# Stores of scan operands begun by ScalarE's queue instead of SyncE's

## The chip, the cores and the metric

The kernel runs on one core of a Trainium2 chip. The core has TensorE (PE, matrix products), VectorE (DVE), ScalarE (ACT), GpSimd (POOL) and SyncE (SP), which here only begins transfers (DMAs). Each engine works through its own list of instructions in order; an instruction waits until the semaphores that it names are high enough, and all behind it on that engine wait too. A DMA is begun by the engine in whose list it stands: `nc.sync.dma_start` is SyncE, `nc.scalar.dma_start` is ScalarE. The metric is the device time in microseconds (us).

## The reference, cut to what matters

One inference step through two layers, over 128 context tokens and 1024 latent tokens: an attention layer with an MLP, and then a bidirectional RWKV-7 layer with an MLP. The change lies in the second layer's time mixing:

```
xr, xw, xk, xv, xa, xg = (h + xx * mu[n] for n in range(6))
r = (xr @ w_rkv[0]).reshape(hs)
k = (xk @ w_rkv[1]).reshape(hs)
v = (xv @ w_rkv[2]).reshape(hs)
...
for d in range(2):
    wlog = -softplus(-(w0[d] + tanh(xw @ w1[d]) @ w2[d])) - 0.5
    decay = exp(-exp(wlog))
    a = sigmoid(a0[d] + (xa @ a1[d]) @ a2[d])
    kd = k * (1.0 + (a - 1.0) * k_a)
    y, sf = wkv_scan(r, decay, kd, v, kk, a, s0[:, d], reverse=(d == 1))
```

The scan is a recurrence over tokens: S = S * w - (S kk) (kk a)^T + v k^T, y = S r, for 16 heads of 64 in each direction.

## The kernel before, in words

All 1152 tokens are held as 9 tiles of 128 or 3 blocks of 384, and as 18 chunks of 64 for the scan. Features lie in 8 groups p8 of 128 (two heads). The RWKV layer has two stages: `rwkv_proj` makes projections and operands, `rwkv_scan` runs the recurrence.

`rwkv_proj` runs a row of dense projections (`dense`, `gemm`, line 1113, tiles rp): for r (`dense(0)`) and for v (`dense(2)`), 24 outputs of 128x384 each, every one 24 matmuls of split weights pwh and pwl. ScalarE copies each out of PSUM (L1118, ro) and begins its store (L1119); for v the block is also transposed on TensorE (L1209, vp), copied (L1211, vt) and stored (L1212). While these run, the generator `operands()` is stepped every second projection. It goes over 8 groups p8 and 3 blocks b, and in each over two directions d: 48 steps. A step is, with the names that the rows show:

- on TensorE two small projections lp (L1176), which give the decay and the rate before their nonlinearities;
- on ScalarE cum (tanh, L1262), ec (L1263) and tha (L1266);
- on VectorE the scan over the chunk (L1264);
- on ScalarE the exponentials en and ec (L1268, L1269), the chunk's decay Dc (L1270) and kd (L1276);
- on GpSimd the two halves of ar (L1272, L1273), kd times k (L1277) and half of bk (L1281); on VectorE tha times kk (L1278) and the other half of bk (L1280);
- on TensorE 48 small products ng of bk and ar (L1292): the diagonal blocks of 32 x 32; on VectorE nt (L1294), their masked copy.

At the start of a block k, kk and r are loaded (L1227, L1247), into a ring of six buffers (tag ld); VectorE scales kk (L1249). After both directions GpSimd adds the two kd (L1300), VectorE multiplies them with r (L1301), and TensorE sums over heads (hst, L1126). Once the third of the inputs of v is mixed, three of four steps keep cum, en, tha and so on in a spare large tile, and the rows then call them es. ar, bk and ld have two, two and six buffers. A step ends with its stores: ar to ard (384 KB, L1274), bk to bkd (384 KB, L1282), nt to nd (64 or 96 KB, L1298), and in the first block of a group also the first two chunks to ndp (32 KB, L1297). That is 48 + 48 + 48 + 16 = 160 stores. After a group's last block, for the first three groups, the diagonal blocks are loaded back (L1346) and inverted on VectorE (L1351, L1352).

`rwkv_scan` later loads ard and bkd (L1433 to L1439) and runs the recurrence.

What stands in which place of an engine's list is decided when the kernel is built, by a planner that plays the program through a model of the chip (`schedule_with_timeline_sim=True`). It also picks the buffers of a ring. So an edit on one engine can move instructions on all.

Of the kernel before, what the change touches and what calls it, by code (L numbers as in the profile page):

```python
# [58 lines left out]
def heads(ap):  # L59

    return ap[:, None].to_broadcast([2, 64, ap.shape[-1]])
# [28 lines left out]
class Net:  # L90
# [932 lines left out]
    def rwkv_proj(self, act, early, pool, pse, ps):  # L1023
        A, S, V, G, T, dma, dr = self.A, self.S, self.V, self.G, self.T, self.dma, self.dr
        KE = (V, G)[KDE]
        NC, NB = TOK // 64, 6
# [95 lines left out]
        def head_sums(x, out):  # L1122

            sp = ps.tile([128, 3, 2], F32, tag="st", name=self.nm("hst"), bufs=1)
            for t in range(3):
                T.matmul(sp[:, t], x[:, t * 128 : (t + 1) * 128], ones2, start=True, stop=True)  # L1126
            V.tensor_copy(out.rearrange("p e t -> p t e"), sp)
# [39 lines left out]
        def second_weights(n, p8):  # L1167

            w = pool.tile([128, 128], F32, tag="w2", name=self.nm("w2"), bufs=4)
            src = A[{1: "rwkv_w2", 4: "rwkv_a2", 5: "rwkv_g2"}[n]][0]  # L1170
            dma(w, (src if n == 5 else src.rearrange("d r n -> (d r) n"))[:, p8 * 128 : p8 * 128 + 128])
            return w

        def second(n, w, b, r):
            p = pse.tile([128, HW], F32, tag="lp", name=self.nm("lp"), bufs=3)[:, 0:TB]
            T.matmul(p, w[r], tl[n, b][r], start=True, stop=True)  # L1176
            return p
# [36 lines left out]
        def etiles():  # L1214

            nonlocal turn
            turn = (turn + 1) % 4 if len(vs) == 3 else 0
            if turn:
                t = self.act_pool.tile([128, KD * HW], F32, tag=f"acta{turn - 1}", name=self.nm("es"))
                it = iter(t[:, i * NB * 65 : (i + 1) * NB * 65] for i in range(6))  # L1220
                return lambda nme, w=TB: next(it)[:, 0:w]
            return lambda nme, w=TB: pool.tile([128, NB * 65], F32, tag="e", name=self.nm(nme), bufs=EB)[:, 0:w]

        def load(src, nme):
            t = pool.tile([128, TB], F32, tag="ld", name=self.nm(nme), bufs=LB)
            if src is not None:
                dma(t, src)  # L1227
            return t

        def operands():  # L1230


            nm = pool.tile([128, 32], F32, name="nm")
            for e in range(2):
                for i in range(2):
                    r = slice(64 * e + 32 * i, 64 * e + 32 * i + 32)
                    dma(nm[r], self.C["gmask"][r, 0, e, 32 * i : 32 * i + 32])
            self.tri = {}
            ndp = self.tri[KD] = dr.tile([KD, 2, 2, 2, 2, 32, 32], F32, name="ndp")
            for p8 in range(KD):  # L1240
                ww, wa = second_weights(1, p8), second_weights(4, p8)
                for b in range(3):
                    ts = slice(b * TB, (b + 1) * TB)
                    cs = slice(b * NB, (b + 1) * NB)
                    k = load(rkd[1][:, p8, ts], "k")
                    kk = load(None, "kk")
                    dma(kk, heads(kkd[p8, :, ts]))  # L1247
                    r = load(rkd[0][:, p8, ts], "r")
                    V.scalar_tensor_tensor(kk, k, self.CB[:, 80 + p8 : 81 + p8], kk, op0=ALU.mult, op1=ALU.mult)  # L1249
                    kds = None  # L1250
                    for d in range(2):
                        etile = etiles()
                        inc = slice(1, 65) if d == 0 else slice(0, 64)
                        exc = slice(0, 64) if d == 0 else slice(1, 65)
                        pad = slice(0, 1) if d == 0 else slice(64, 65)
                        last = slice(64, 65) if d == 0 else slice(0, 1)
                        st = 1 if d == 0 else -1
                        cw, ca = 48 + d * 8 + p8, 64 + d * 8 + p8
                        ec = etile("ec", NB * 65).rearrange("p (c t) -> p c t", t=65)
                        c_ = etile("cum", NB * 65).rearrange("p (c t) -> p c t", t=65)  # L1260
                        G.memset(ec[:, :, pad], 0.0)
                        S.activation(c64(c_[:, :, :].rearrange("p c t -> p (c t)")[:, 0:TB]), c64(second(1, ww, b, row(d))), AF.Tanh, bias=hb[:, cw : cw + 1], scale=0.5)  # L1262
                        S.activation(ec[:, :, inc], c64(flat(c_)[:, 0:TB]), AF.Copy, scale=-0.5 * KAP, bias=-0.5 * KAP)  # L1263
                        V.tensor_tensor_scan(flat(c_)[:, ::st], flat(m01), flat(ec)[:, ::st], 0.0, op0=ALU.mult, op1=ALU.add)  # L1264
                        tha = etile("tha")
                        S.activation(tha, second(4, wa, b, row(d)), AF.Tanh, bias=hb[:, ca : ca + 1], scale=0.5)  # L1266
                        en = etile("en")
                        S.activation(c64(en), c_[:, :, inc], AF.Exp, scale=-1.0)  # L1268
                        S.activation(flat(ec), flat(c_), AF.Exp)  # L1269
                        S.activation(self.Dc[:, p8, d, cs, None], c_[:, :, last], AF.Exp)  # L1270
                        ar = pool.tile([128, 2, NB, 64], F32, tag="ar", name=self.nm("ar"), bufs=2)
                        G.tensor_tensor(ar[:, 0], c64(kk), ec[:, :, exc], op=ALU.mult)  # L1272
                        G.tensor_tensor(ar[:, 1], c64(r), ec[:, :, inc], op=ALU.mult)  # L1273
                        dma(self.ard[d][p8, :, :, cs], ar)  # L1274
                        kd = etile("kd")
                        S.activation(kd, tha, AF.Identity, scale=hb[:, 88 + p8 : 89 + p8], bias=oka[:, p8 : p8 + 1])  # L1276
                        KE.tensor_tensor(kd, kd, k, op=ALU.mult)  # L1277
                        V.scalar_tensor_tensor(tha, tha, 1.0, kk, op0=ALU.add, op1=ALU.mult)  # L1278
                        bk = pool.tile([128, 2, NB, 64], F32, tag="bk", name=self.nm("bk"), bufs=2)
                        V.scalar_tensor_tensor(bk[:, 0], c64(tha), 0.5, c64(en), op0=ALU.mult, op1=ALU.mult)  # L1280
                        (V, G)[BKE].tensor_tensor(bk[:, 1], c64(kd), c64(en), op=ALU.mult)  # L1281
                        dma(self.bkd[d][p8, :, :, cs], bk)  # L1282
                        if b == 0 and d == 0:
                            nd = dr.tile([2, NC - 2, 2, 2, 32, 32], F32, name=self.nm("nd"))

                        ng = ps.tile([128, NB, 32], F32, tag="ng", name=self.nm("ng"), bufs=1)
                        for j in range(NB):
                            for e in range(2):
                                x, z = (bk, ar) if d == 0 else (ar, bk)
                                for i in range(2):  # L1290
                                    t = slice(32 * i, 32 * i + 32)
                                    T.matmul(ng[64 * e + 32 * i : 64 * e + 32 * i + 32, j], x[row(e), 0, j, t], z[row(e), 0, j, t], start=True, stop=True, tile_position=(64 * e, 64 * e + 32 * i))  # L1292
                        nt = etile("nt", TB // 2).rearrange("p (c t) -> p c t", t=32)
                        V.tensor_tensor(nt, ng, nm[:, None, :].to_broadcast([128, NB, 32]), op=ALU.mult)  # L1294
                        m = 2 if b == 0 else 0
                        if m:
                            dma(ndp[p8, d].rearrange("c e i s t -> (e i s) c t"), nt[:, 0:m])  # L1297
                        dma(nd[d, b * NB + m - 2 : b * NB + NB - 2].rearrange("c e i s t -> (e i s) c t"), nt[:, m:])  # L1298
                        kds = kd if d == 0 else (kds, kd)
                    G.tensor_tensor(kds[0], kds[0], kds[1], op=ALU.add)  # L1300
                    V.scalar_tensor_tensor(kds[0], r, self.CB[:, 96 + p8 : 97 + p8], kds[0], op0=ALU.mult, op1=ALU.mult)  # L1301
                    head_sums(kds[0], bss[:, p8, :, 3 * b : 3 * b + 3])
                    if b == 2:
                        self.tri[p8] = nd
                        if p8 < PI:
                            for _ in self.invert(pool, p8):
                                pass
                    yield
# [584 lines left out]
```

## Time and profile before

| | us |
|---|---|
| median of 3 runs (4411.51 to 4431.69) | 4413.0 |
| profiled execution, its own time | 4424.38 |
| span of its trace, first to last instruction | 4422.6 |
| busy in the span: TensorE, VectorE, ScalarE, GpSimd | 3968.7, 2764.0, 1713.0, 1231.5 |

The operands are made from about 2263 to 2755 us of the span, some 490 us. The profile has rows by stretch (how long each engine was busy), waits (which engine idled for which instruction of which other), and a timeline (start in us, duration in us, engine, line, operation, output<-input, and in brackets the idle time just before with its cause). SPq and ACTq are DMAs begun by SyncE and ScalarE; the time of such a row is that of beginning the transfer, not of moving the data. PE clock in the tables is the granted clock of TensorE as a share of full speed.

### The profile page before, as it was taken

The page shows a single profiled execution, that of the slowest core. Times are in us where ns is not written, and L with a number is a line of the kernel's source. Part 1 is how long each engine was busy: PE and PEld are TensorE (multiplying, and loading weights), DVE is VectorE, ACT ScalarE, POOL GpSimd, SP SyncE. Part 2 cuts the span into 40 slices and gives each one's busy share as a digit, 9 for nine tenths or more (in the row PEclk, how much of TensorE's full clock was granted, in tenths as well). Part 3 has the DMA queues.
Part 4 walks back from the last instruction along what each step waited for, and adds up shares of the span by engine and source line. Part 5 has one row for each costly group of instructions (what it writes and reads, how often), then busy time and mean ns, then how long its engine had stood idle before and what let it go on. Part 6 is the DMA issues. An engine that isn't in the chain of part 4 may idle for free.

```text
span 4422.6 us, 78577 instructions
## 1 busy us (share of the span) xinstructions
PE 3968.7 (90%) x30058; PEld 3378.6 (76%) x30058; DVE 2764.0 (62%) x5837; ACT 1713.0 (39%) x4041; POOL 1231.5 (28%) x1519
## 2 busy tenths in 40 slices
PE   6989998879999999989987676898999799999998
PEld 5767777667788888868876555676777589999997
DVE  6856878865766666675157884677643564444445
ACT  5436776543211111133344444454554342222222
POOL 1223557750000000023256565344444200000001
PEclk8999999889999999989998777899999799999999
DMA  4444223223222222222235666766653511111112
GB/s 164 127 139 123 77 73 87 83 70 122 78 72 72 67 76 78 67 101 49 96 114 151 169 202 170 172 153 150 158 138 92 180 59 47 48 39 48 39 39 100
DMA packets 558520, 452.35 MB, mean 102 GB/s; under 512 B 191303, under 2 KB 529215, under 8 KB 556991
## 3 DMA queue, kind: packets, MB, share of 16 engines
q1 hardware_dynamic: 533472, 413.62, 32.6%
q10 hardware_dynamic: 24672, 33.71, 2.3%
q8 instruction: 238, 3.90, 0.4%
q14 instruction: 138, 1.12, 0.1%
HBM read 323.45 MB, written 123.76 MB: 101 GB/s over the span
## 4 chain that ended last, share of the span: by engine, by line
PE 34%; DVE 7%; DMA 6%; issue 3%; ACT 3%; POOL 2%; SPq 1%; ACTq 0%; DVEq 0%; POOLq 0%
PE mp L938 9%; PE acc L958 9%; PE rp L1113 5%; PE gp L1455 3%; PE acc L906 2%; DMA kk<-kkd 1%; DMA ta<-td 1%; DVE iv L1352 1%; DVE ivt L1351 1%; DVE h_b L1070 1%; PE yp L1564 1%; DMA v<-vd 1%; PE cp L1548 1%; PE yp L1545 1%; PE cp L1532 1%
## 5 line engine op out<-in xcount | busy, mean ns | idle before, releaser
L958 PE MATMUL acc<-w2h,f 128*128 128x512 f32 x2304 | 733.8, 392 | 7.4 <-ACT f L837 4.5
L938 PE MATMUL mp<-h_b,w1h 128*128 128x384 f32 x1536 | 521.6, 340 | 0.0
L938 PE MATMUL mp<-h_a,w1h 128*128 128x384 f32 x1536 | 516.8, 337 | 0.8 <-ACT h L302 0.7
L938 PE MATMUL mp<-h_a,w1l 128*128 128x384 f32 x1536 | 516.6, 336 | 0.0
L958 PEld LDWEIGHTS acc<-w2h,f 128*128 128x128 f32 x2304 | 432.0, 188 | 104.1 <-ACT f L837 6.0
L958 PE MATMUL acc<-w2l,f 128*128 128x512 f32 x1152 | 451.4, 392 | 0.0
L964 DVE TENSOR_TENSOR acc<-acc,acc 128x1024 f32<-128x1024 f32 x270 | 328.9, 1218 | 138.0 <-PE acc L958 135.9
L1455 PE MATMUL gp<-ar,bk 128*64 128x192 f32 x2304 | 288.5, 352 | 23.6 <-DMA bk<-bkd 11.4
L662 POOL TENSOR_TENSOR ptl<-pt,pth 128x512 fp32r<-128x512 f32 x192 | 248.4, 1295 | 217.9 <-DVE pth L661 126.2
L938 PEld LDWEIGHTS mp<-h_a,w1h 128*128 128x128 f32 x1536 | 288.3, 188 | 7.0 <-issue 2.0
L938 PEld LDWEIGHTS mp<-h_b,w1h 128*128 128x128 f32 x1536 | 288.7, 188 | 4.2 <-issue 0.7
L938 PEld LDWEIGHTS mp<-h_a,w1l 128*128 128x128 f32 x1536 | 288.9, 188 | 0.1
L940 ACT ACTIVATE mt<-mp 128x384 f32<-128x384 f32 x192 | 94.0, 490 | 498.0 <-PE mp L938 495.9
L1113 PE MATMUL rp<-mxh,pwh 128*128 128x384 f32 (+2 forms) x720 | 267.5, 372 | 12.4 <-POOL pwh L1104 6.6
L990 POOL TENSOR_TENSOR acc<-acc,mraw 128x1024 f32<-128x1024 f32 x6 | 15.4, 2562 | 899.7 <-DVE mrv L112 893.0
L1113 PE MATMUL rp<-h_b,pwh 128*128 128x384 f32 (+2 forms) x720 | 259.5, 361 | 2.5 <-DVE h_b L1070 2.5
L1113 PE MATMUL rp<-mxh,pwl 128*128 128x384 f32 (+2 forms) x720 | 256.8, 359 | 1.3 <-POOL pwl L1101 1.3
L1793 POOL MEMSET h_a<- 128x8 f32 x4 | 0.3, 113 | 901.9 <-PE mp L938 901.9
L958 PEld LDWEIGHTS acc<-w2l,f 128*128 128x128 f32 x1152 | 216.2, 188 | 44.7 <-issue 3.1
L942 DVE TENSOR_TENSOR mf<-mt 128x384 f32<-128x384 f32 x192 | 106.3, 554 | 213.0 <-ACT mt L940 212.9
L1456 DVE TENSOR_TENSOR g<-gp,gm 128x384 f32<-128x384 f32 x288 | 157.7, 554 | 109.7 <-PE gp L1455 101.5
L1455 PEld LDWEIGHTS gp<-ar,bk 128*64 128x64 f32 x2304 | 172.1, 145 | 47.0 <-issue 16.5
(439 smaller groups left out, 9568.3 us busy)
## 6 DMA issues: line engine op xcount, KB each, us to landing
mraw<-in_mlp_w_dram SPq DMA_DIRECT2D x64, 1024.0 KB
adaw<-in_w_ada_dram SPq DMA_DIRECT2D x80, 512.0 KB
bkd<-bk SPq DMA_DIRECT2D x48, 384.0 KB
ard<-ar SPq DMA_DIRECT2D x48, 384.0 KB
q<-QSd SPq DMA_DIRECT2D x256, 64.0 KB
ar<-ard SPq DMA_DIRECT2D x40, 384.0 KB
praw<-in_rwkv_w_rkv_dram SPq DMA_DIRECT2D x24, 512.0 KB
x1d<-acc SPq DMA_DIRECT2D x18, 512.0 KB
```

The lines of the kernel that those rows point to most:

```text
L662: (V if w < 4 else G).tensor_tensor(c["l"][:, g : g + w, o], t["tp", g][:, 0:w], f32(c["h"][:, g : g + w, o]), op=ALU.subtract)
L906: T.matmul(ps[t][:, hf], oact[b].v[u][:, k, cols], wo[k][y][:, hf * 512 : hf * 512 + 512], start=k == 0 and i == 0, stop=k == KD - 1 and i ...
L938: T.matmul(p, x[:, k, :], act[b].v[y][:, k], start=k == 0 and i == 0, stop=k == KD - 1 and i == 2)
L940: S.activation(t, p, AF.Relu)
L942: V.tensor_tensor(f, t, t, op=ALU.mult)
L958: T.matmul(p[:, hf], x[:, cols], y[:, n], start=j == 0 and i == 0, stop=j == 1 and i == 2)
L964: V.tensor_tensor(a, a, pf, op=ALU.add)
L1070: V.tensor_tensor(lo[:, k], m, f32(hi[:, k]), op=ALU.subtract)
L1113: T.matmul(p, x[:, k, :], a[y][:, k], start=k == 0 and i == 0, stop=k == KD - 1 and i == 2)
L1351: V.tensor_tensor(tmp, nb_[:, s, s + 1 : 32, None].to_broadcast([128, n, s + 1]), iv[:, s, None, 0 : s + 1].to_broadcast([128, n, s + 1]), ...
L1455: T.matmul(gp[row(x), j].rearrange("p (a t) -> p a t", t=64), bk[e][:, x, q + j], ar[:, :, q + j], start=True, stop=True, tile_position=(0 ...
L1456: V.tensor_tensor(g[:, e].rearrange("p j a t -> p j (a t)"), gp, gm[:, d, e, None].to_broadcast([128, 2, 192]), op=ALU.mult)
```

## The change

Four kinds of store in `operands()`, those of ar, bk and nt (lines 1274, 1282, 1297, 1298), are begun by ScalarE (`self.dma_s`) instead of SyncE (`dma`). Data, sizes and destinations stay the same.

```diff
@@ -1271,7 +1271,7 @@
                         ar = pool.tile([128, 2, NB, 64], F32, tag="ar", name=self.nm("ar"), bufs=2)
                         G.tensor_tensor(ar[:, 0], c64(kk), ec[:, :, exc], op=ALU.mult)
                         G.tensor_tensor(ar[:, 1], c64(r), ec[:, :, inc], op=ALU.mult)
-                        dma(self.ard[d][p8, :, :, cs], ar)
+                        self.dma_s(self.ard[d][p8, :, :, cs], ar)
                         kd = etile("kd")
                         S.activation(kd, tha, AF.Identity, scale=hb[:, 88 + p8 : 89 + p8], bias=oka[:, p8 : p8 + 1])
                         KE.tensor_tensor(kd, kd, k, op=ALU.mult)
@@ -1279,7 +1279,7 @@
                         bk = pool.tile([128, 2, NB, 64], F32, tag="bk", name=self.nm("bk"), bufs=2)
                         V.scalar_tensor_tensor(bk[:, 0], c64(tha), 0.5, c64(en), op0=ALU.mult, op1=ALU.mult)
                         (V, G)[BKE].tensor_tensor(bk[:, 1], c64(kd), c64(en), op=ALU.mult)
-                        dma(self.bkd[d][p8, :, :, cs], bk)
+                        self.dma_s(self.bkd[d][p8, :, :, cs], bk)
                         if b == 0 and d == 0:
                             nd = dr.tile([2, NC - 2, 2, 2, 32, 32], F32, name=self.nm("nd"))
 
@@ -1294,8 +1294,8 @@
                         V.tensor_tensor(nt, ng, nm[:, None, :].to_broadcast([128, NB, 32]), op=ALU.mult)
                         m = 2 if b == 0 else 0
                         if m:
-                            dma(ndp[p8, d].rearrange("c e i s t -> (e i s) c t"), nt[:, 0:m])
-                        dma(nd[d, b * NB + m - 2 : b * NB + NB - 2].rearrange("c e i s t -> (e i s) c t"), nt[:, m:])
+                            self.dma_s(ndp[p8, d].rearrange("c e i s t -> (e i s) c t"), nt[:, 0:m])
+                        self.dma_s(nd[d, b * NB + m - 2 : b * NB + NB - 2].rearrange("c e i s t -> (e i s) c t"), nt[:, m:])
                         kds = kd if d == 0 else (kds, kd)
                     G.tensor_tensor(kds[0], kds[0], kds[1], op=ALU.add)
                     V.scalar_tensor_tensor(kds[0], r, self.CB[:, 96 + p8 : 97 + p8], kds[0], op0=ALU.mult, op1=ALU.mult)
```


The planner runs anew, so the lists of all engines differ from about the sixth operand step to the end of the scan. Three places are shown; the numbers behind names tell tiles apart.

ScalarE, steps two and three (the two directions of the second block, tiles 22138 and 22194), before:

```order
L1266 ACTIVATE tha_22145<-lp_22146,hb 128x384
L1263 ACTIVATE ec_22137<-cum_22138 128x6x64
L1268 ACTIVATE en_22149<-cum_22138 128x384
L1269 ACTIVATE ec_22137<-cum_22138 128x390
L1270 ACTIVATE Dc<-cum_22138 128x6
L1276 ACTIVATE kd_22157<-tha_22145,oka,hb 128x384
L1100 CAST pwh_22734<-praw_22732 128x1024
L1118 COPY ro_22281<-rp_22256 128x384
L1119 DMA rkd_19665<-ro_22281 128x384
L1262 ACTIVATE cum_22194<-lp_22196,hb 128x384
L1266 ACTIVATE tha_22201<-lp_22202,hb 128x384
L1263 ACTIVATE ec_22193<-cum_22194 128x6x64
```


and now:

```order
L1266 ACTIVATE tha_22145<-lp_22146,hb 128x384
L1297 DMA ndp<-nt_22057 128x2x32
L1298 DMA nd_21974<-nt_22057 128x4x32
L1263 ACTIVATE ec_22137<-cum_22138 128x6x64
...
L1282 DMA bkd_19674<-bk_22161 256x1x384
L1262 ACTIVATE cum_22194<-lp_22196,hb 128x384
L1266 ACTIVATE tha_22201<-lp_22202,hb 128x384
L1298 DMA nd_21974<-nt_22190 128x6x32
L1263 ACTIVATE ec_22193<-cum_22194 128x6x64
```


The stores ndp and nd of the step before stand between L1266 and L1263 of the first of them, and the store of its bk stands ahead of L1262, L1266, nd and L1263 of the second.

SyncE, the loads of the third block (k_22318, kk_22320, r_22322) before, among the stores of the first:

```order
L1227 DMA k_22318<-rkd_19666 128x384
L1274 DMA ard_19673<-ar_22020 256x1x384
L1247 DMA kk_22320<-kkd 128x1x384
L1282 DMA bkd_19675<-bk_22028 256x1x384
L1227 DMA r_22322<-rkd_19665 128x384
L1297 DMA ndp<-nt_22057 128x2x32
L1298 DMA nd_21974<-nt_22057 128x4x32
L1274 DMA ard_19672<-ar_22153 256x1x384
```


and now:

```order
L1091 DMA praw_22732<-in_rwkv_w_rkv_dram 128x8x128
L1091 DMA praw_22948<-in_rwkv_w_rkv_dram 128x8x128
L1227 DMA k_22318<-rkd_19666 128x384
L1247 DMA kk_22320<-kkd 128x1x384
L1227 DMA r_22322<-rkd_19665 128x384
L1091 DMA praw_23396<-in_rwkv_w_rkv_dram 128x8x128
L1227 DMA k_22603<-rkd_19666 128x384
L1171 DMA w_4602_23263<-in_rwkv_w_dram 128x128
```


Between the loads only loads of weights (praw, w) are left.

TensorE, behind the last dense projection (rp_26578), before:

```order
L1113 MATMUL rp_26578<-mxh_24057,pwl_26170 128x384
L1292 MATMUL ng_26708<-bk_26704,ar_26697 32x32 x24
L1126 MATMUL hst_26859<-ones_19676,es_26750 128x2 x3
L1176 MATMUL lp_26929<-lt_20112,w_5188_26622 128x384
L1209 MATMUL vp_26606<-ident,ro_26603 64x128 x3
L1209 MATMUL vp_26613<-ident,ro_26603 64x128 x3
L1134 MATMUL rtp_26980<-ident,bss 72x128
L1292 MATMUL ng_26774<-ar_26763,bk_26770 32x32 x24
L1292 MATMUL ng_26829<-bk_26825,ar_26817 32x32 x24
L1292 MATMUL ng_26895<-ar_26884,bk_26891 32x32 x24
L1292 MATMUL ng_26946<-bk_26942,ar_26935 32x32 x24
```


and now (small projections, head sums and transposes left out in part):

```order
L1113 MATMUL rp_26578<-mxh_24057,pwl_26170 128x384
L1292 MATMUL ng_26656<-ar_26644,bk_26651 32x32 x24
...
L1292 MATMUL ng_26708<-bk_26704,ar_26697 32x32 x24
L1176 MATMUL lp_26873<-lt_19907,w_5187_26620 128x384
...
L1176 MATMUL lp_26924<-lt_19907,w_5187_26620 128x384
L1292 MATMUL ng_26774<-ar_26763,bk_26770 32x32 x24
L1176 MATMUL lp_26929<-lt_20112,w_5188_26622 128x384
L1292 MATMUL ng_26829<-bk_26825,ar_26817 32x32 x24
...
L1292 MATMUL ng_26895<-ar_26884,bk_26891 32x32 x24
L1292 MATMUL ng_26946<-bk_26942,ar_26935 32x32 x24
```


Before, five groups of ng stand behind the last projection and one lp; now six and seven.

## Rows read from the trace of the kernel before

**Rows 1.** Table by stretches (busy us of PE, PEld, DVE, ACT, POOL; clock, DMA)
```profile
2285.00:2375.00 90.00, 80.61 (x714) 67.75 (x712) 43.69 (x75) 33.12 (x70) 46.74 (x45) 0.96 0.55 159
2375.00:2600.00 225.00, 160.09 (x1572) 124.64 (x1572) 202.95 (x304) 114.25 (x246) 144.40 (x146) 0.79 0.60 167
2600.00:2755.00 155.00, 115.44 (x1434) 94.49 (x1432) 77.26 (x113) 74.48 (x167) 97.91 (x108) 0.81 0.63 186
```

**Rows 2.** The same table, GpSimd's line 1272 alone, one per step
```profile
2285.00:2375.00 90.00, 7.46 (x8) 0.96 0.55 159
2375.00:2600.00 225.00, 23.36 (x21) 0.79 0.60 167
2600.00:2755.00 155.00, 18.32 (x18) 0.81 0.63 186
```

**Rows 3.** Waits, 2250 to 2756 us (total us, times, longest)
```profile
ACT en L1268 <- DVE cum L1264: 58.6, 15, 7.6
ACT es L1268 <- DVE es L1264: 51.9, 18, 7.6
DVE kk L1249 <- DMA kk<-kkd: 48.3, 14, 9.5
```

**Rows 4.** Timeline, loads of kk, their readers (start, us, engine, line, [idle before])
```profile
2264.17 0.59 SPq L1247 DMA_DIRECT2D kk<-kkd  x1
...
2271.35 0.62 DVE L1249 SCALAR_TENSOR_TENSOR kk<-k,CB,kk 128x384 f32<-128x384 f32 x1 [9.46 <-DMA kk<-kkd]
...
2288.30 1.32 POOL L1277 TENSOR_TENSOR kd<-kd,k 128x384 f32<-128x384 f32 x1
...
2289.65 0.54 SPq L1247 DMA_DIRECT2D kk<-kkd  x1
...
2297.15 0.62 DVE L1249 SCALAR_TENSOR_TENSOR kk<-k,CB,kk 128x384 f32<-128x384 f32 x1 [4.83 <-DMA kk<-kkd]
...
2647.38 1.37 POOL L1277 TENSOR_TENSOR es<-es,k 128x384 f32<-128x384 f32 x1 [2.21 <-ACT es L1276]
...
2650.20 0.61 SPq L1247 DMA_DIRECT2D kk<-kkd  x1
```

**Rows 5.** Stores by tile (begin ns min/median/max)
```profile
L1274 SPq DMA_DIRECT2D ard<-ar x48: 512/522/2498, 2275.2 to 2747.1; - x48
...
L1282 SPq DMA_DIRECT2D bkd<-bk x48: 513/534/5072, 2274.5 to 2747.9; - x48
...
L1298 SPq DMA_DIRECT2D nd<-nt x25: 365/460/1637, 2282.3 to 2741.0; - x25
```

**Rows 6.** Timeline of the serial stretch, ScalarE, VectorE, GpSimd and SyncE
```profile
2291.89 0.52 ACT L1263 ACTIVATE ec<-cum 128x384 f32<-128x384 f32 x1
...
2297.68 0.35 DVE L1294 TENSOR_TENSOR nt<-ng,nm 128x192 f32<-128x192 f32 x1
...
2298.02 0.96 DVE L1264 TENSOR_TENSOR_SCAN cum<-m,ec 128x390 f32<-128x390 f32 x1
...
2298.49 0.46 SPq L1298 DMA_DIRECT2D nd<-nt  x1
...
2302.62 0.58 ACT L1262 ACTIVATE cum<-lp,hb 128x384 f32<-128x384 f32 x1 [0.65 <-DVE bk L1280]
...
2303.10 0.57 ACT L1266 ACTIVATE tha<-lp,hb 128x384 f32<-128x384 f32 x1
...
2305.74 1.00 POOL L1281 TENSOR_TENSOR bk<-kd,en 128x384 f32<-128x384 f32 x1
...
2306.77 0.52 SPq L1282 DMA_DIRECT2D bkd<-bk  x1
...
2306.82 0.97 DVE L1264 TENSOR_TENSOR_SCAN cum<-m,ec 128x390 f32<-128x390 f32 x1 [3.08 <-POOL ec L1261]
```

**Rows 7.** Timeline of TensorE at the end of the stage
```profile
2734.92 0.34 PE L1113 MATMUL rp<-mxh,pwl 128*128 128x384 f32 x1
...
2746.41 0.86 PE L1292 MATMUL ng<-bk,ar 64*32 64x32 f32 x48 [4.37 <-DVE bk L1280]
```


## The prediction

> **What bounds the kernel now.** The change touches one stage, the making of the operands, so I read the profile in this order: the table by stretches of that stage, then the waits of VectorE and ScalarE in it, then the timeline around single loads and stores. The reader is to see three things.
>
> First, the stage has no single bound [rows 1]. From 2285 to 2375 us TensorE is busy 80.6 of 90 us and VectorE only 43.7. From 2375 to 2600 us it is the reverse: VectorE is busy 203 of 225 us, since it also inverts diagonal blocks and mixes the third input there, and TensorE falls to 160. From 2600 to 2755 us nobody is full: TensorE 115 of 155 us, GpSimd 98, VectorE 77, ScalarE 74. What paces that last stretch is the chain of one step through ScalarE, VectorE, GpSimd and TensorE. A step is one direction of one block; 8, 21 and 18 of the 48 steps lie in the three stretches [rows 2], so the last runs at 155 / 18 = 8.6 us per step.
>
> Second, ScalarE is idle for long, and waits mostly for the scan on VectorE: 58.6 + 51.9 us before the exponentials of L1268 [rows 3]. That is the only room in which it can begin stores free of charge. Third, VectorE does wait for loads: 48.3 us in 14 waits for kk [rows 3]. Whether SyncE's stores are to blame for that decides what the change can gain.
>
> **The gain: are the loads held by stores?** The load of kk at 2289.65 us begins 0.03 us after GpSimd's L1277, which reads the tile of k two blocks back, ends (2288.30 + 1.32) [rows 4]. It was waiting for its buffer, not for the store in front of it, and so it is in two of the next three blocks. Later it differs: the load at 2650.20 us begins 1.45 us after the L1277 of its block ends (2647.38 + 1.37), and a store of a diagonal block was begun just ahead of it [rows 4]. So the gain lies between nothing and 24 blocks x 1.45 = 35 us. I take a quarter of the blocks as held, as in the first stretch, and 14 of 24 waited for: 24 x 0.25 x 1.45 x 14 / 24 = 5 us. The VectorE wait that stays is landing time: the kk load begun at 2289.65 us is used at 2297.15, 7.5 us later, whoever begins the stores.
>
> Does a load land sooner when the stores are in another queue? At 2264.17 us, with no store begun just before, kk took until 2271.35, 7.2 us; behind a store it took 7.5 [rows 4]. The difference is 0.3 us, and I count nothing for it. The Trainium skill ("DMA: Bandwidth & Descriptors", section "Issuing engines are not separate DMA queues") says that DMAs begun by different engines run on the same 16 DMA engines and interleave, and that a second issuing engine saves only the sequencer's time; this speaks against a gain in landing. Another section of that page ("Queues, rings and completion order") has SP's and ACT's transfers in separate rings that take turns, by which a load would no longer queue behind a store. By the first rule the sum stays as it is, by the second it would lose 24 x 0.3 = 7 us more. The 7.2 beside 7.5 us bears out the first rather than the second.
>
> **The cost: 160 stores on ScalarE.** Each step's stores are one of ar (median 0.522 us to begin), one of bk (0.534) and one of the diagonal blocks (0.460), 1.5 us per step [rows 5]; the 16 that are left are a second, smaller store of diagonal blocks in 16 steps. Beginning them is not the main thing; waiting for their data in ScalarE's order is. Four cases:
>
> *The serial stretch, 2285 to 2375 us, 8 steps.* In the new order the store of the diagonal blocks of a step stands ahead of L1263 of the next one, and on VectorE the scan of the next step stands right behind the product that this store waits for. Before, L1263 had run at 2291.89 us and the scan started at 2298.02, as soon as the product (2297.68 + 0.35) was out [rows 6]. Now ScalarE begins the store after 2298.03 (0.46), then runs L1263 (0.52), with two handovers of about 0.1: the scan starts about 1.2 us later. In the other direction of a block the store of bk stands ahead of L1262, L1266 and L1263. GpSimd's bk ends at 2306.74, the store took 0.52, the three activations follow at 0.48 us each (the distance of the starts of L1262 and L1266): 2306.77 + 0.52 + 3 x 0.48 + 0.15 = 2308.9, where the scan started at 2306.82 before [rows 6]. That is 2.1 us. A block loses 3.3 us and the four blocks 13. Lower end 0, if TensorE (80.6 of 90 us busy) is what paces here and the lag is made good later; I take 13, because the lag is in the new order too: at the end of the stage one step more than before is left behind the last projection.
>
> *2375 to 2600 us, 21 steps.* The same delay, 3.3 / 2 = 1.65 us a step, is at most 35 us. It lies beside VectorE's own work, which fills 203 of 225 us. What is not covered is VectorE's idle share, 22 / 225 = 0.10: 3 us. If that cover were gone it would be all 35.
>
> *2600 to 2755 us, 18 steps.* At most 18 x 1.65 = 30 us. Here VectorE, which runs behind ScalarE in the chain, is idle half the time (78 of 155 us), so I take half: 15 us. Against more speaks that in this stretch ScalarE works on two or three steps at once, and a store often waits for a step that ScalarE has long left.
>
> *The tail.* After the last projection five products of diagonal blocks were left before, and six now, with seven small projections between them where there was one. The last projection ended at 2735.26 us and the last of the five products began at 2746.41: 11.2 us for four distances, 2.8 us each [rows 7]. One more: 3 us.
>
> SyncE's side costs nothing: it keeps its loads and loses its stores. In the scan stage that follows the planner puts many instructions in another order; I see no reason for a sign there, and put 10 us either way into the range.
>
> **Sum.** 13 + 3 + 15 + 3 - 5 = 29 us. It is made against the profiled execution: 4424.4 us, of which 4422.6 are the span, gives 4453. That execution was 11.4 us above the median of 4413.0, and since nothing in the sum depends on what made it slower, the forecast is 4413 + 29 = **4442 us**. The ends are 0 and 13, 0 and 35, 0 and 30, and a gain of 0 to 35; their half widths (7, 18, 15, 18) added in squares make 30 us, of which 25 should hold 8 times in 10: its own range is 4417 to 4467.
>
> **The rivals.**
>
> *No change.* The stores fall into the 110 us that ScalarE waits for scans, and the lag of the first stretch is worked off in the last, where VectorE has 78 us of idle time. For it: the idle time is there. Against it: in the first stretch the store stands exactly between the two instructions of the cycle. Time: 4413 us, give or take 10.
>
> *Faster: loads were held.* If every block's kk was held as the one at 2650.20 us, and ScalarE has room for all stores, 35 us go: 4378 us. For it: VectorE's 48.3 us of waiting. Against it: three of the four blocks looked at in the first stretch waited for their buffer.
>
> *Much slower: ScalarE becomes the bound.* In the last stretch it is busy 74.5 / 18 = 4.1 us per step; 1.5 us of stores make 5.6 of 8.6, and the waits inside now block copies out of PSUM as well. From 3 us of such waits per step on, ScalarE decides, and then all delays count: 1.65 x 47 = 78 us, and 3 for the tail: 4494 us. For it: single waits of ScalarE for a scan were 7.6 us long [rows 3], so data do come late. Against it: the planner placed each store where it expected the data.
>
> **How the numbers follow.** The forecast has 0.48, no change 0.27, faster 0.16, much slower 0.09. A measurement of this kernel can tell about 0.5% from no change, 22 us: 4391 and 4435. Of the forecast 0.12 lies below 4435. So slower is 0.36 + 0.09 = 0.45, the same 0.27 + 0.12 = 0.39, faster 0.16. The range leaves out about half of the faster case and the much slower one: 4384 to 4480.
>
> **What would show it.** Right: in the profile after, ScalarE waits at L1263 or L1262 right behind stores in the first stretch, the two scans of a block (2298.02 and 2306.82 before, 8.8 us apart [rows 6]) stand about 11 us apart there, the stage ends 20 to 45 us later, and VectorE's wait for kk stays above 35 us. Wrong: the wait for kk falls to half (loads were held), or the stage is as long as before although ScalarE waits at stores (its idle time covered them), or the difference lies in the scan stage.

## The result, and the profile after

| | before | after |
|---|---|---|
| median of 5 runs, us | 4419.22 (4411.51 to 4431.69) | 4450.73 (4446.41 to 4457.41) |
| ratio, 95% interval | | 1.0074, 1.0059 to 1.0088 |
| span of the profiled execution, us | 4422.6 | 4455.6 |

The change makes the kernel 31.5 us slower, 0.74%. The same three stretches of the changed kernel, in the columns of [rows 1]:

```profile
2285.00:2375.00 90.00, 79.85 (x691) 68.04 (x690) 40.66 (x68) 29.56 (x61) 43.14 (x42) 0.91 0.51 152
2375.00:2600.00 225.00, 155.94 (x1505) 126.51 (x1504) 187.31 (x283) 109.89 (x237) 133.67 (x134) 0.80 0.56 157
2600.00:2755.00 155.00, 116.57 (x1378) 90.23 (x1382) 88.48 (x126) 76.12 (x171) 98.90 (x105) 0.78 0.60 182
```

and the steps in them, by GpSimd's line 1272 as in [rows 2]:

```profile
2285.00:2375.00 90.00, 5.64 (x6) 0.91 0.51 152
2375.00:2600.00 225.00, 20.42 (x19) 0.80 0.56 157
2600.00:2755.00 155.00, 18.47 (x19) 0.78 0.60 182
```

No computing engine has become fuller, but for VectorE in the last stretch (88 us against 77); beginning transfers is not counted as busy in these rows. In the first stretch six steps begin instead of eight, in the second 19 instead of 21, and VectorE, which was idle for 22 us of the second, is now idle for 38. So the chain of a step is longer, while the instructions that compute are the same. The waits of the same time as in [rows 3], with one of GpSimd (total us, times, longest):

```profile
DVE kk L1249 <- DMA kk<-kkd: 77.1, 17, 9.1
...
ACT es L1268 <- DVE es L1264: 28.5, 14, 5.0
...
POOL es L1261 <- DMA nd<-es: 20.7, 4, 9.1
...
ACT en L1268 <- DVE cum L1264: 19.7, 14, 7.3
```

ScalarE's waits for the scan have fallen from 110.5 to 48.2 us; it now stands at its stores instead. VectorE's wait for kk, which the change was to shorten, has grown from 48.3 to 77.1 us. The places at which ScalarE stands, in the timeline of the serial stretch that answers to [rows 6] (ACTq is a transfer begun by ScalarE):

```profile
2290.73 0.57 ACT L1266 ACTIVATE tha<-lp,hb 128x384 f32<-128x384 f32 x1
...
2296.02 0.35 DVE L1294 TENSOR_TENSOR nt<-ng,nm 128x192 f32<-128x192 f32 x1
...
2296.40 0.38 ACTq L1297 DMA_DIRECT2D ndp<-nt  x1
...
2296.81 0.48 ACTq L1298 DMA_DIRECT2D nd<-nt  x1
...
2297.34 0.53 ACT L1263 ACTIVATE ec<-cum 128x384 f32<-128x384 f32 x1 [6.04 <-DVE bss L1127]
...
2297.97 0.97 DVE L1264 TENSOR_TENSOR_SCAN cum<-m,ec 128x390 f32<-128x390 f32 x1 [1.53 <-ACT ec L1263]
...
2305.69 0.99 POOL L1281 TENSOR_TENSOR bk<-kd,en 128x384 f32<-128x384 f32 x1
...
2306.71 0.53 ACTq L1282 DMA_DIRECT2D bkd<-bk  x1
...
2307.29 0.58 ACT L1262 ACTIVATE cum<-lp,hb 128x384 f32<-128x384 f32 x1 [3.40 <-POOL ec L1261]
...
2308.27 0.53 ACT L1263 ACTIVATE ec<-cum 128x384 f32<-128x384 f32 x1
...
2308.88 0.97 DVE L1264 TENSOR_TENSOR_SCAN cum<-m,ec 128x390 f32<-128x390 f32 x1 [5.21 <-ACT ec L1263]
```

(The bracket of L1263 counts all the time in which ScalarE does not compute, the begins too.) After L1266 ScalarE does nothing for 5.1 us, until VectorE has made nt at 2296.37. Then it begins two stores and runs L1263, and VectorE's scan starts 1.6 us after nt, where it had followed at once [rows 6]. In the other direction GpSimd's bk ends at 2306.68, its store and three activations follow, and the scan starts 2.2 us later. Added up in the timeline over the whole stage (2263 to 2785 us), ScalarE stands still for 17.0 us ahead of the stores of ar, 22.3 ahead of bk, and 58.8 ahead of ndp and nd, 98 us in all, and spends 85 us on beginning them. Another 10.5 us ahead of the very first store of bk start at 2261.5 us, before that window.

Where the lag arises can be followed by one instruction, VectorE's scan: the second, the 9th, the 16th, the 31st and the last of the stage, then the scan stage's first product gp and its last yp on TensorE. Before:

```profile
2283.67 1.48 DVE L1264 TENSOR_TENSOR_SCAN cum<-m,ec 128x390 f32<-128x390 f32 x1 [1.84 <-ACT ec L1263]
...
2371.22 0.96 DVE L1264 TENSOR_TENSOR_SCAN cum<-m,ec 128x390 f32<-128x390 f32 x1
...
2478.13 0.96 DVE L1264 TENSOR_TENSOR_SCAN cum<-m,ec 128x390 f32<-128x390 f32 x1
...
2606.30 1.70 DVE L1264 TENSOR_TENSOR_SCAN es<-m,es 128x390 f32<-128x390 f32 x1
...
2742.60 1.27 DVE L1264 TENSOR_TENSOR_SCAN es<-m,es 128x390 f32<-128x390 f32 x1 [1.63 <-ACT es L1263]
...
2761.44 2.82 PE L1455 MATMUL gp<-ar,bk 128*64 128x192 f32 x16 [9.71 <-DMA bk<-bkd]
...
3455.95 0.64 PE L1564 MATMUL yp<-g,mu 128*64 128x64 f32 x6
```

and after:

```profile
2281.54 1.20 DVE L1264 TENSOR_TENSOR_SCAN cum<-m,ec 128x390 f32<-128x390 f32 x1 [2.09 <-ACT ec L1263]
...
2377.88 0.96 DVE L1264 TENSOR_TENSOR_SCAN cum<-m,ec 128x390 f32<-128x390 f32 x1
...
2496.08 0.96 DVE L1264 TENSOR_TENSOR_SCAN cum<-m,ec 128x390 f32<-128x390 f32 x1
...
2624.59 1.77 DVE L1264 TENSOR_TENSOR_SCAN es<-m,es 128x390 f32<-128x390 f32 x1
...
2757.08 1.75 DVE L1264 TENSOR_TENSOR_SCAN es<-m,es 128x390 f32<-128x390 f32 x1
...
2780.27 2.83 PE L1455 MATMUL gp<-ar,bk 128*64 128x192 f32 x16 [9.37 <-DMA bk<-bkd]
...
3487.76 0.64 PE L1564 MATMUL yp<-g,mu 128*64 128x64 f32 x6
```

The differences are -2.1, +6.7, +18.0, +18.3, +14.5, +18.8 and +31.8 us. So the first stretch costs 8.8 us, the second 11.6, the last gives back 3.8, the tail costs 4.3, which makes 21 in the operands. Another 13.0 us come in the scan stage, in which no store was moved.

Nearly all of the second stretch's loss (11.3 us) is there by the 16th scan, and from then on the lag does not grow. 7.3 us come between the 9th and the 10th scan and 9.5 more by the 11th, of which 5.5 are made good again. Between the 9th and the 10th VectorE's share of mixing the third input (L1068, L1070) is, before and after (the stretch, its length, busy us and count of these instructions; then clock and DMA):

```profile
2371.22:2384.30 13.08, 0.55 (x1) 0.87 0.55 159
2377.88:2398.24 20.36, 10.04 (x14) 0.95 0.24 77
```

One of these instructions stood ahead of the 10th scan before, and 14 do now. That they are what holds this scan up is argued and not shown.

The tail is seen on TensorE, and answers to [rows 7]: the last projection, the first group of ng behind it, and the last group.

```profile
2727.03 0.34 PE L1113 MATMUL rp<-mxh,pwl 128*128 128x384 f32 x1
...
2727.30 0.62 PE L1292 MATMUL ng<-ar,bk 64*32 64x32 f32 x48
...
2764.39 0.87 PE L1292 MATMUL ng<-bk,ar 64*32 64x32 f32 x48 [0.85 <-POOL ar L1272]
```

The projections end 7.9 us earlier than before, and the ng drag on for 37.9 us behind them, where it had been 12: six groups with five distances of 7.4 us on average, where it had been five groups 2.8 us apart. TensorE did not wait for late projections; the operands fell behind.

### The profile page after: what moved, and what is told of

It reads as the page before. It is cut to its first block, busy times and chain, and to the rows that moved or that the text cites. A ratio compares the mean times of both kernels' runs of the same rounds, so it can differ in the third digit from the quotient of the medians.

```text
span 4455.6 us, 78490 instructions
## 1 busy us (share of the span) xinstructions
PE 3980.2 (89%) x30058; PEld 3388.0 (76%) x30058; DVE 2767.0 (62%) x5837; ACT 1711.0 (38%) x4041; POOL 1231.9 (28%) x1519
## 5 line engine op out<-in xcount | busy, mean ns | idle before, releaser
L1113 PE MATMUL rp<-mxh,pwh 128*128 128x384 f32 (+2 forms) x720 | 266.5, 370 | 11.6 <-POOL pwh L1104 6.1
```

The lines of the kernel that those rows point to most:

```text
L1113: T.matmul(p, x[:, k, :], a[y][:, k], start=k == 0 and i == 0, stop=k == KD - 1 and i == 2)
```

## Experiments

Theory A is the prediction's: ScalarE waits, in its own order, for the data of the stores. B: the stores lie in another queue, land later and free buffers later. C: the planner's new order is the cause. D: the time to begin 160 transfers. Beside each median stand two lengths from the one profiled execution: "operands", from VectorE's first product with kk (L1249) to the first gp, 490.1 us before and 511.5 after; and "scan", from there to the end of the last yp, 695.1 us before and 708.1 after. How much these lengths differ between executions of one kernel was not measured, and an order that moves no store (e4, below) shifts the operands by 4.2 us; a difference of some 5 us or less says little by itself. The kernel before ran beside the others with medians of 4419.99 (e1 to e4), 4423.46 (e5 to e8) and 4419.22 us (e9 to e12).

**One store at a time.** e1 moves the diagonal blocks, e2 bk, e3 ar:

```diff
 e1  -dma(ndp[...], nt[:, 0:m]); dma(nd[...], nt[:, m:])
     +self.dma_s(ndp[...], nt[:, 0:m]); self.dma_s(nd[...], nt[:, m:])
 e2  -dma(self.bkd[d][p8, :, :, cs], bk)
     +self.dma_s(self.bkd[d][p8, :, :, cs], bk)
 e3  -dma(self.ard[d][p8, :, :, cs], ar)
     +self.dma_s(self.ard[d][p8, :, :, cs], ar)
```

> Only the stores of the diagonal blocks (ndp and nd, 64 of the 160) are begun by ScalarE. In the whole change ScalarE stood still for 58.8 us ahead of these stores, 22.3 ahead of bkd and 17.0 ahead of ard. Theory A (waiting for the data of a store in ScalarE's list costs the time): about 60% of the loss of 31.5 us, so +19 us, and ScalarE's waits ahead of L1297 and L1298 stay near 59 us. Rival B (the transfers now lie in ScalarE's queue and land later, and buffers come free later): the two large stores cost, this one is small, +0 to +5 us. Rival C (the planner's new order alone makes the difference): any value between -15 and +30, not tied to the waits.

> Only the stores of bk (48 of 160) are begun by ScalarE. Theory A: 22.3 of 98 us of waits, so about +7 us. Rival B (the queue): 48 of 96 large stores, +13 us. Rival C (the planner's order): any value between -15 and +30.

> Only the stores of ar (48 of 160) are begun by ScalarE. Theory A: 17.0 of 98 us of waits, so about +5 us. Rival B (the queue): 48 of 96 large stores, +13 us. Rival C (the planner's order): any value between -15 and +30.

| | median | ratio, interval | operands | scan | ScalarE still ahead of the stores |
|---|---|---|---|---|---|
| e1 nd, ndp | 4429.28 | 1.0017, 1.0008 to 1.0026 | 495.7 | 700.2 | 67.7 |
| e2 bkd | 4439.85 | 1.0039, 1.0027 to 1.0052 | 498.6 | 704.9 | 60.4 |
| e3 ard | 4414.83 | 0.9992, 0.9982 to 1.0002 | 488.9 | 693.5 | 19.8 |

Theory A's shares were wrong, since they were taken from the waits of the whole change: bk alone makes ScalarE wait nearly as long as the diagonal blocks alone do (10.5 of its 60.4 us lie ahead of the very first store), and costs no less. By the ratios e1 costs 7.5 us, where A had 19, and e2 17, where A had 7. The order is A's, though: the store with short waits costs nothing that can be measured. By B ar, as large as bk, should have cost as much, and it does not. Nor is it D alone: e3 begins 48 stores on ScalarE, 26 us in all, and loses nothing (ns: shortest, median, longest):

```profile
L1274 ACTq DMA_DIRECT2D ard<-ar x48: 520/534/642, 2273.1 to 2745.1; - x48
```

So a begin does not cost its length wherever it stands.

**Another order of the same instructions.** e4 is the kernel before, e7 the changed one, each with two lines exchanged:

```diff
-V.scalar_tensor_tensor(bk[:, 0], c64(tha), 0.5, c64(en), op0=ALU.mult, op1=ALU.mult)
 (V, G)[BKE].tensor_tensor(bk[:, 1], c64(kd), c64(en), op=ALU.mult)
+V.scalar_tensor_tensor(bk[:, 0], c64(tha), 0.5, c64(en), op0=ALU.mult, op1=ALU.mult)
```

> No store is moved: the two lines that make the halves of bk (L1280 on VectorE, L1281 on GpSimd) are written in the other order. Neither needs the other, each engine has the same instructions, but the planner runs anew and orders 1887 of TensorE's instructions otherwise. Theories A and B: within 5 us of the kernel before. Rival C: 15 us or more away from it, either way.

> The whole change, and the two lines of bk written in the other order, so that the planner makes another order of the same instructions. If the loss is due to the moved stores (Theory A or B): +25 to +38 us against before, and the scan stage again some 13 us longer. If the scan's 13 us are an accident of this one order: the operands again 19 to 21 us later at the scan's first product, but the scan stage within 6 us of before, so +13 to +27.

e4: 4415.89 us, 0.9987 (0.9977 to 0.9997), operands 485.9, scan 689.1. e7: 4439.16 us, 1.0037 (1.0024 to 1.0049), operands 509.8, scan 689.4. The first gp and the last yp of e7:

```profile
2780.39 2.83 PE L1455 MATMUL gp<-ar,bk 128*64 128x192 f32 x16 [9.63 <-DMA bk<-bkd]
...
3469.13 0.64 PE L1564 MATMUL yp<-g,mu 128*64 128x64 f32 x6
```

With the stores on ScalarE the operands are 21 us longer in the first order, and 24 in the second (e7 against e4); the scan's 13 us are gone in the second. So C is not the cause of the operands' loss, but it is part of the 31.5 us: that much depends on which order the planner happened to make. Between e4 and e7, whose sources differ by the moved stores alone, lie 0.50% by the ratios, 22 us. Whether moved stores make a long scan stage more likely stays open: of the seven kernels here that move stores it takes 700 to 708 us in four (the change, e1, e2, e10), and in the seven others never more than 695.5.

**Waiting without beginning, beginning without waiting, and both.** The stores stay with SyncE. e5 has the copies, e6 transfers of constants, written behind L1262 and L1276, e9 a transfer written behind each copy:

```diff
 e5  dma(self.ard[d][p8, :, :, cs], ar)
    +S.copy(seen[:, 0:2], ar[:, :, 0, 0])        # and so behind bkd and nd
 e6  S.activation(kd, tha, AF.Identity, ...)
    +self.tc.keep_in_program_order(self.dma_s(spare[p8, b, d, 2], nm))   # two more behind L1262
 e9 +S.copy(seen[:, 0:2], ar[:, :, 0, 0])
    +self.tc.keep_in_program_order(self.dma_s(spare[p8, b, d, 0], nm))   # and so behind bkd and nd
```

> All stores stay with SyncE. ScalarE instead reads one or two elements a row of ar, bk and nt in each step (three tiny copies, 144 in all), so it has to wait for the same data in its own order, but begins none of these transfers. Theory A (waiting in ScalarE's order): most of the loss of 31.5 us is here, +15 to +30, with some 90 us of standing still ahead of the three copies. Rival B (the queue that the transfers lie in): nothing, within 6 us of before. Rival D (the time that beginning 160 transfers takes on ScalarE, 85 us): little, +3 to +8, since the copies take less time to run.

> All stores stay with SyncE. ScalarE begins three other transfers in each step (144 in all, 16 KB each, from a tile of constants into unused memory), fixed behind L1262 (two) and behind L1276 (one): their data are always ready, so they cost only the time to begin them. Theory A: within 8 us of before. Rival B: nothing, since these transfers are small. Rival D: 144 x 0.4 = 58 us on ScalarE, two of three on the path to the scan: 48 x 0.8 = 38 us at most, so +15 or more.

> All stores stay with SyncE. In each step ScalarE makes the three tiny copies of e5 and right behind each begins a small transfer of constants (16 KB, into unused memory), so it both waits where the moved stores waited and spends the time to begin a transfer, 144 times. What the operands take, from VectorE's first product with kk to the scan stage's first product, was 490.1 us before, 495.3 with the copies alone, 505.1 with the beginnings alone, and 511.5 and 509.8 in the two orders of the whole change. Theory A+D (waiting and beginning, both on ScalarE, and nothing else): 508 to 515 us, and 15 to 30 us on the whole. Rival B (the queue that the real stores lie in): below 503 us.

| | median | ratio, interval | operands | scan |
|---|---|---|---|---|
| e5 look | 4430.14 | 1.0016, 1.0004 to 1.0028 | 495.3 | 692.4 |
| e6 begin | 4435.15 | 1.0029, 1.0019 to 1.0039 | 505.1 | 691.9 |
| e9 both | 4450.48 | 1.0072, 1.0057 to 1.0087 | 516.5 | 695.5 |

ScalarE's copies in e5, grouped (busy us, mean ns, then the idle time ahead of them and what ended it):

```profile
L1285 ACT COPY seen<-bk 128x2 f32<-128x2 f32 x48 | 9.1, 190 | 47.5 <-DVE bk L1282 25.4 <-POOL bk L1283 9.4 <-POOL ec L1262 9.0
L1276 ACT COPY seen<-ar 128x2 f32<-128x2 f32 x48 | 9.1, 190 | 18.3 <-POOL ar L1274 16.1 <-ACT vt L1211 0.8 <-ACT ro L1118 0.8
L1302 ACT COPY seen<-nt 128x1 f32<-128x1 f32 x25 | 4.8, 190 | 37.3 <-DVE nt L1297 37.3
L1302 ACT COPY seen<-es 128x1 f32<-128x1 f32 x23 | 4.4, 191 | 21.0 <-DVE es L1297 19.7 <-DVE bss L1127 0.9 <-ACT ro L1118 0.4
```

These rows add up to 124 us, with other begins counted as idle. By the measure used above ScalarE stands still here for 114 us, about as long as in the change (109 with the first wait for bk), and the operands lose only 5.2 us. Beginning alone, at places that may be worse than those of the moved stores, costs them 15.0 us. (The places hold in part: by their starts 15, 22 and 10 of e6's three times 48 transfers stand right behind the activation that they were written behind, and 76 of e9's 144 right behind their copy.) With both, 26.4 us are lost, as many as with the real stores or more, though these all lie in SyncE's queue. So B explains nothing that is left to explain. Over the whole stage A's waits are the smaller part (5.2 us), and D's begins the larger: 15.0 us alone, and 21.2 on top of the waits (516.5 - 495.3).

The 5.2 us hide two movements, though. From the second scan to the 9th the waits alone lose 5.5 us, the begins alone 6.6, both 9.6, and the change 8.8. At the 31st scan the waits alone are 15.0 us behind and the begins alone 15.2; by the last one e5 has made good 10.3 of them, and e6 0.4. So in the serial stretch waiting and beginning cost about the same. Whether e5's gain at the end belongs to the waits or to the planner's order stays open: e4, which moves nothing, gains 5.3 us there, and e3 8.2.

As to what was expected: e5 is 7 us slower by its ratio, below A's 15; e6 12.8, a little below D's 15; e9's 516.5 and 31 us lie just above the ranges of A and D together. Not all of e9's 31 us are the operands': in e5 and e9 the stage also begins 5 to 6 us later than before, for which no cause was looked for.

**Another engine begins them.** In e10 it is GpSimd, for all four kinds:

```diff
-self.dma_s(self.ard[d][p8, :, :, cs], ar)
+self.nc.gpsimd.dma_start(self.ard[d][p8, :, :, cs], ar)
```

> The 160 stores are begun by GpSimd instead, so SyncE only loads, as in the change, and ScalarE keeps its own list. If freeing SyncE is worth something in itself and ScalarE alone made the loss: -10 to 0 us. If any computing engine that begins them pays as ScalarE did: GpSimd is busy 98 of 155 us in the last stretch, and would wait for VectorE's half of bk and for nt, +15 to +40.

4495.16 us, 1.0177 (1.0160 to 1.0195), operands 556.3, scan 701.1. SyncE is as free as in the change, and the loss, 78 us, is more than twice as large and far above the 15 to 40 that were expected. The begins on GpSimd (ns: shortest, median, longest):

```profile
L1282 POOL DMA_DIRECT2D bkd<-bk x48: 672/756/996, 2271.8 to 2810.0; - x48
```

Each takes longer than on ScalarE (median 534 ns for bk), counts as busy time of the engine, and stands among the products that make ar and bk.

**Load buffers.** e8 is the kernel before, e12 the changed one, with kk in other buffers; e11 is e8 with e4's exchanged lines:

```diff
-kk = load(None, "kk")
+kk = pool.tile([128, TB], F32, tag="lt", name=self.nm("kk"), bufs=9)
```

> The kernel before, with kk taken out of the six load buffers and put into those of the low-rank tiles (tag lt), of which three are free by then: the six are left for k and r alone, three blocks deep instead of two. If loads were held by buffers and not by SyncE's stores: VectorE's wait for kk falls from 48.3 us to below 20, and the time by 5 to 25 us. If they were held by the stores: both stay.

> The kernel before with both edits that were faster by themselves: kk in the buffers of the low-rank tiles (e8, 0.9979) and the two lines of bk swapped (e4, 0.9987). If they add up: 0.9966, -15 us. If e4 was only another order, whose gain the planner does not find again in another program: the operands as in e8 (486 us) and the scan stage anywhere from 689 to 708 us, so -10 to +10.

> The whole change and kk in the buffers of the low-rank tiles. If the changed kernel's longer wait for kk (77.1 us instead of 48.3) is a matter of buffers: the operands take 5 us or more less than its 510 to 511 us. If the wait only follows from the chain running late behind ScalarE: within 3 us of 510.

e8: 4415.29 us, 0.9979 (0.9967 to 0.9992), operands 486.2, scan 695.1. e11: 4415.72 us, 0.9998 (0.9987 to 1.0008), 484.9 and 692.9. e12: 4438.03 us, 1.0047 (1.0034 to 1.0061), 505.8 and 694.0. VectorE's waits in e8:

```profile
DVE kk L1249 <- DMA k<-rkd: 40.8, 10, 7.9
...
DVE kk L1249 <- DMA kk<-kkd: 23.6, 7, 9.2
```

The expected fall of the wait did not come: now it is k that comes last, and the two make 64 us. The operands gain 3.9 us in e8 and 5.7 in e12 (against the change), but only 1.0 in e11 (against e4). So buffers hold loads a little at most, with SyncE full of stores or without them. (e12's 5.7 us just meet the 5 that were named for a matter of buffers, but are hardly more than an order shifts.) By its interval e8 is faster than the kernel before, by 9 us; e11, which has the same edit, did not bear that out.

## Why the prediction was right, and where its steps were not

It forecast 4442 us, 29 above the median of the runs shown; 31.5 were measured, inside its own range (4417 to 4467). The mechanism was right: stores in ScalarE's list delay the next scan. In the serial stretch even the sizes hold: 1.2 us were forecast behind nt and 1.6 measured (ndp adds 0.4), 2.1 behind bk and 2.2 measured, and the two scans stand 10.9 us apart, forecast about 11. But the near agreement of the sum is luck in part: the 29 us were meant for the operands, which lost 21, and 13 came in the scan stage, for which nothing was forecast. In the other order (e7) the whole loss is 16 us. Of its own signs, the wait for kk and the scans 11 us apart came true; the stage ended 18 us later by the last ng, a little less than the 20 to 45 named; and a part of the difference does lie in the scan stage, a sign of being wrong. Step by step:

- *First stretch, 13 us.* 8.8 measured. The lag grows from scan to scan, with two small steps back, as worked out, and part of it is hidden.
- *2375 to 2600 us, 3 us.* 11.6 measured. This is the step that failed most plainly: VectorE's own work was taken as cover for 90% of the delay, all along. Up to the 16th scan it was none: 11.3 us were lost there, as much as seven steps at the prediction's 1.65 us; more of VectorE's mixing stands ahead of the 10th scan than before, and VectorE's idle time in the stretch grew from 22 to 38 us. From the 16th scan on the lag stayed, as if covered.
- *2600 to 2755 us, 15 us, and the tail, 3 us.* -3.8 and +4.3 by the last scan. The half that was taken does not show; the lag that was there stayed about as large. In other orders without a loss this stretch gives back as much or more (e3 8.2 us, e4 5.3), so the split between it and the stretch before is not firm. In the tail the groups of ng stand 7.4 us apart, not 2.8.
- *The gain, 5 us.* None. From its begin to VectorE's use kk took 7.47 us before and 7.79 after (medians of 24; of those that VectorE waited for, 7.30 in 14 and 7.69 in 17), so a load was not ready sooner for having SyncE's queue to itself. The rule of the Trainium skill ("DMA: Bandwidth & Descriptors", "Issuing engines are not separate DMA queues") that transfers run on the same 16 DMA engines whoever begins them agrees with this. As the prediction read the Trainium skill's section "Queues, rings and completion order" on the same page, by which SP and ACT have separate rings that take turns, the time would have fallen.
- *"Beginning them is not the main thing; waiting for their data in ScalarE's order is."* Not borne out: over the stage e5 loses 5.2 us for 114 us of waiting, e6 15.0 for 144 begins, and in the serial stretch the two cost about the same. A likely reason why so little of the waiting counts, argued and not shown: ScalarE's next activation mostly needs the same chain that it waits for at the store, so the wait replaces one that comes anyway (110.5 us at the scan fell to 48.2), while a begin in the chain comes on top.
- *Ten us either way for the scan stage.* 13 came, just outside, and they are gone in e7, which moves the same stores; so they depend on the order. What in that order makes the scan longer, and whether the moved stores favour such orders, stays open.

Of the rivals, "no change" fell because the idle time of ScalarE hid only part: 98 + 85 us were put on it, and the operands lost 21. "Much slower" did not come: ScalarE's waits at the scan gave way first. "Loads were held" is refuted by the wait for kk, which grew.

## What to carry to other kernels

An engine that idles half its time is not a free place for beginning transfers when it is one link of a chain: a begin that stands between two instructions of the chain lengthens it (e6), waiting for the data of a store can lengthen it too (e5, serial stretch), and the stores of ar, which wait little, cost nothing that can be measured (e3). Before stores are moved away from a queue that only begins transfers, look at whether a load in it waits for the store ahead of it or for its buffer. Where a planner orders everything anew, run the change in two orders: here one harmless exchange of lines moved the result from +31.5 to +16 us, and the length of the stage concerned was the steadier measure (511.5 and 509.8 us).

## What was not expected of the hardware

Beginning a transfer of 16 KB took ScalarE more than half as long as one of 384 KB: 0.33 to 0.45 us (medians at e6's three places) against 0.53. Begun by GpSimd a 384 KB store took 0.76 us of the engine. And 114 us of standing still on one engine in a stage of 490 us cost that stage 5 us (e5).
